# Second layer's attention: one matmul of 96 rows in place of three of 16 rows for the meta keys

## The chip, the cores and the metric

The kernel runs on one core of one Trainium2 chip. The metric is the device time of one execution in microseconds. A core has several engines that run side by side, each with its own queue of instructions in order: PE (TensorE, the matmuls; its weight loads are listed as PEld), DVE (VectorE), ACT (ScalarE), POOL (GpSimd) and SP (SyncE, which issues most of the DMAs). Matmul results land in PSUM, everything else on the chip lies in SBUF; both have 128 partitions, called rows here. A matmul sums over the rows of its two operands: the one that is loaded first as weights (`lhsT`) and the one that is streamed (`rhs`), one column after the other.

## The reference

The input is 512 tokens of width 1024, in front of which 16 learned meta tokens are put. Three layers follow: a gated delta rule, a latent attention with 16 heads, and a block with pooling, dilated attention and a feed-forward part. The change lies in the second, whose attention is:

```python
def causal_block_attention(q_nope, q_rope, k_nope, k_rope, v):
    ...
        s = (jnp.einsum('bqhd,bkhd->bhqk', qn_b, k_nope, preferred_element_type=jnp.float32)
             + jnp.einsum('bqhr,bkr->bhqk', qr_b, k_rope, preferred_element_type=jnp.float32))
        q_pos = blk * Q_BLOCK + jnp.arange(Q_BLOCK)
        s = jnp.where(q_pos[:, None] >= k_pos[None, :], s * scale, -jnp.inf)
        p = jax.nn.softmax(s, axis=-1)
        return jnp.einsum('bhqk,bkhd->bqhd', p.astype(v.dtype), v)
```

The keys are the 16 meta tokens and the 512 real ones. Keys and values of all heads come from one latent of width 128 (`c_kv`), so that the kernel can weigh the latent itself with the softmax weights and bring in each head's value matrix afterwards.

## The kernel before, in words

Everything is computed in full float32 precision by split products. A float32 tensor is cut in two by `cut` (line 75): ScalarE copies it into the matmuls' rounded float32 format (the high part), then VectorE subtracts that from the original (the low part). A product of two cut tensors is three matmuls into the same PSUM tile, `split_mm` (line 67): high by high (line 68), high by low (line 71), low by high (line 72). The fourth, low by low, is left out.

`Second.run` is the second layer. `latents` prepares the shared latent: beside the projections it is normalised, transposed in five chunks (the 16 meta tokens, then four times 128 tokens) and cut into `cthi` and `ctlo`, in which chunk 0 uses only rows 0 to 15.

Then the attention loop runs over 64 steps, 16 heads by 4 blocks of 128 queries. Different parts of it work on different steps at a time: `scores` on step i, `softmax_scale` on i - 1, `flip` on i - 2, `weigh` on i - 4 and `values` on i - 5, the last two once for two blocks (a half, 256 queries); `prep_a` and `prep_b` prepare the next head's queries.

- `scores`: matmuls into the PSUM tile `sc`; VectorE scales, masks and finds the extremum (line 1390), ScalarE takes the exponential (line 1395) into `p`; `softmax_scale` divides by the sum, on VectorE (line 1403) and GpSimd (line 1404).
- `flip`: PE transposes `p`, the 16 meta columns into `trm` (line 1726; a tile of which there is one, shared by the two blocks of a half) and the others into `ptr` (line 1729). These are cut into the pair `pt`, and `trm`, once both blocks are in it, into the pair `pm`, 16 rows by 256 queries.
- `weigh`: the latent weighed by the softmax weights. First the split product with the meta keys, three matmuls with 16 rows and 256 columns (`pm` by chunk 0 of `cthi`, `ctlo`), then the split products with the 2 or 4 blocks of real keys, 128 rows each, all into one PSUM tile. The result is cut into `oc`.
- `values`: `oc` by the head's value matrix, times the gate `sz`, cut into `ghi`/`glo`, the input of the layer's output projection.

Where the working tiles lie: `keep` is a pool that lives through the layer; `wk` is opened for the attention loop, after the pool with the layer's input (`h1hi`, `h1lo`) has been closed, on the same memory. `ones` is a constant tile of ones, 128x128.

The order of each engine's instructions is not that of the program text: when the kernel is built, a list scheduler orders them by the program's order as priority and by a simulated timeline (`schedule_with_timeline_sim=True`), except where the text keeps an order. So matmuls of `weigh`, `values`, `scores` and `flip` of neighbouring steps stand between one another in PE's queue.

Of the kernel before, what the change touches and what calls it, by code (L numbers as in the profile page):

```python
# [13 lines left out]
F32R = mybir.dt.float32r  # L14
AF = mybir.ActivationFunctionType
# [5 lines left out]
P = 128  # L21
D = 1024
KT = 8
META = 16
# [42 lines left out]
def split_mm(nc, ps, whi, wlo, xhi, xlo, start, stop, side=None):  # L67
    first = nc.tensor.matmul(ps, lhsT=whi, rhs=xhi, start=start, stop=False)  # L68
    if side is not None:
        side.hold(first)  # L70
    nc.tensor.matmul(ps, lhsT=whi, rhs=xlo, start=False, stop=False)  # L71
    nc.tensor.matmul(ps, lhsT=wlo, rhs=xhi, start=False, stop=stop)  # L72


def cut(nc, hi, lo, src, gain=None, engine=None):

    if gain is None:
        nc.scalar.activation(hi, src, AF.Copy)  # L78
        (engine or nc.vector).tensor_tensor(out=lo, in0=src, in1=hi.bitcast(F32), op=ALU.subtract)  # L79
    else:  # L80
        nc.scalar.activation(hi, src, AF.Copy, scale=gain)
        nc.vector.scalar_tensor_tensor(
            out=lo, in0=src, scalar=gain, in1=hi.bitcast(F32), op0=ALU.mult, op1=ALU.subtract
        )
# [1382 lines left out]
class Second:  # L1467
# [59 lines left out]
    def run(self, mixed):  # L1527
        e = self.e
        tc, nc, a, dram, pj, wts, ident, ones, vcol = (
            e.tc, e.nc, e.a, e.dram, e.pj, e.wts, e.ident, e.ones, e.vcol  # L1530
        )
# [10 lines left out]
        keep = ks_.enter_context(tc.tile_pool(reuse_waits="tile", name="l2", bufs=1, side="right"))  # L1542
# [3 lines left out]
        nc.scalar.dma_start(causal, a["causal"])  # L1546
        chi = keep.tile([P, T1], F32R, name="chi")
        clo = keep.tile([P, T1], F32R, name="clo")
        cthi = keep.tile([P, 5, P], F32R, name="cthi")
        ctlo = keep.tile([P, 5, P], F32R, name="ctlo")  # L1550
        khi = keep.tile([P, T1], F32R, name="krhi")
        klo = keep.tile([P, T1], F32R, name="krlo")
        nsc_q = keep.tile([P, 4], F32, name="nsc_q")
# [7 lines left out]
        def latents():  # L1561
            c = tp_.tile([P, T1], F32, tag="c1", name="c")
            sq = tp_.tile([P, T1], F32, tag="c2", name="csq")
            rc = tp_.tile([P, T1], F32, tag="c3", name="rc")
            nc.vector.tensor_tensor(out=c, in0=ckr[:, 0], in1=rs1, op=ALU.mult)
            nc.scalar.activation(sq, c, AF.Square)
            yield

            ps = tr_tile([P, 2, 4], "qms")
            for b in range(4):  # L1570
                bs = slice(P * b, P * b + P)
                nc.tensor.matmul(
                    ps[:, 0, b:b + 1], lhsT=acc[:, META + P * b:META + P * b + P], rhs=ones[:, 0:1], start=True, stop=True
                )
                for m in range(2):
                    nc.tensor.matmul(
                        ps[:, 1, b:b + 1], lhsT=lsq[:, m, bs], rhs=ones[:, 0:1], start=(m == 0), stop=(m == 1)
                    )
            t = tp_.tile([P, 2, 4], F32, name="qt")
            nc.vector.tensor_scalar(  # L1580
                out=t[:, 0], in0=ps[:, 0], scalar1=EPS / D, scalar2=EPS * EPS, op0=ALU.mult, op1=ALU.add
            )
            nc.vector.tensor_scalar(out=t[:, 1], in0=ps[:, 1], scalar1=1.0 / 256, scalar2=None, op0=ALU.mult)
            nc.vector.tensor_add(t[:, 1], t[:, 1], t[:, 0])
            nc.gpsimd.tensor_tensor(out=nsc_q, in0=t[:, 1], in1=e.half_pow, op=ALU.pow)
            nc.vector.tensor_scalar(out=nsc_q, in0=nsc_q, scalar1=-(192 ** -0.5), scalar2=None, op0=ALU.mult)
            yield
            for s in HALVES:
                token_rs(e, rc[:, s], sq, s, P, 1.0, gap=4.5)
            yield  # L1590
            yield
            nc.vector.scalar_tensor_tensor(
                out=rc, in0=c, scalar=vcol("kv_lat"), in1=rc, op0=ALU.mult, op1=ALU.mult
            )
            cut(nc, chi, clo, rc)
            yield
            for c in range(5):
                t0, n = CHUNKS[c]
                ws = slice(0, P) if c == 0 else slice(t0, t0 + P)
                ps = tr_tile([P, P], "ctp")  # L1600
                nc.tensor.transpose(ps, rc[:, ws], ident)
                cut(nc, cthi[0:n, c], ctlo[0:n, c], ps[0:n])
            yield

            kr = tp_.tile([P, T1], F32, tag="c1", name="kr")
            kx = tp_.tile([P, T1], F32, tag="c2", name="kx")
            nc.vector.tensor_tensor(out=kr, in0=ckr[:, 1], in1=rs1, op=ALU.mult)
            for b in range(4):
                o = b ^ 1
                nc.sync.dma_start(kx[32 * b:32 * b + 32], kr[32 * o:32 * o + 32])  # L1610
            sgn = tp_.tile([P, T1], F32, name="sgn")
            nc.scalar.dma_start(sgn, a["sin_signed"])
            yield
            nc.vector.tensor_mul(kr, kr, cos)
            nc.gpsimd.tensor_mul(kx, kx, sgn)
            yield
            nc.vector.tensor_add(kr, kr, kx)
            cut(nc, khi, klo, kr)
            yield
# [34 lines left out]
        def prep_b(h):  # L1654
# [6 lines left out]
            q_abs[h] = qa  # L1661

        side = latents()
        for h in range(16):
            if h in (2, 5, 8, 11):
# [32 lines left out]

        ws_ = ExitStack()
        wk = ws_.enter_context(tc.tile_pool(reuse_waits="tile", name="l2_work", bufs=2))  # L1700

        def scores(h, b):
            n = META + P * (b + 1)
            qs = slice(P * b, P * b + P)
            qa, qr = q_abs[h], qr_t[h // 4]
            sc = []
            for s in ([slice(0, n)] if n <= 512 else [slice(0, n // 2), slice(n // 2, n)]):
                ps = psm.tile([P, 512], F32, tag="sc", name="sc", bufs=2)[:, :s.stop - s.start]
                split_mm(nc, ps, qa[0][:, qs], qa[1][:, qs], chi[:, s], clo[:, s], True, False)
                nc.tensor.matmul(ps, lhsT=qr[:, h % 4, qs], rhs=khi[:, s], start=False, stop=False)  # L1710
                nc.tensor.matmul(ps, lhsT=qr[:, h % 4, qs], rhs=klo[:, s], start=False, stop=True)
                sc.append(ps)
            live[h, b] = softmax_exp(e, wk, sc, causal[:, T1 - n:], None, nsc_q[:, b:b + 1])

        def flip(h, b):

            p, _, _ = live.pop((h, b))
            half, j = divmod(b, 2)
            if j == 0:
                o = pts[h, half] = Env()  # L1720
                o.pt = [wk.tile([P, 4, 256], F32R, tag=f"pt{i}", name=f"pt{i}") for i in range(2)]
                o.pm = [wk.tile([META, 256], F32R, tag=f"pm{i}", name=f"pm{i}") for i in range(2)]
                o.tm = psm.tile([META, 256], F32, tag="trm", name="trm")
            o = pts[h, half]
            js = slice(P * j, P * j + P)
            nc.tensor.transpose(o.tm[:, js], p[:, 0:META], ident)
            tr = tr_tile([P, 4, P], "ptr")
            for k in range(b + 1):
                nc.tensor.transpose(tr[:, k], p[:, META + P * k:META + P * k + P], ident)  # L1729
            cut(nc, o.pt[0][:, 0:b + 1, js], o.pt[1][:, 0:b + 1, js], tr[:, 0:b + 1])  # L1730
            if j == 1:
                cut(nc, o.pm[0], o.pm[1], o.tm)

        def weigh(h, half):

            o = pts[h, half]
            ps = pj.tile([P, 512], F32, tag="pj", name="pj_t")[:, :256]
            split_mm(nc, ps, cthi[0:META, 0], ctlo[0:META, 0], o.pm[0], o.pm[1], True, False)
            nk = 2 * half + 2
            for k in range(nk):  # L1740
                s = slice(P if k == nk - 1 else 0, 256)
                split_mm(
                    nc, ps[:, s], cthi[:, k + 1], ctlo[:, k + 1], o.pt[0][:, k, s], o.pt[1][:, k, s], False, k == nk - 1
                )
            o.oc = [wk.tile([P, 256], F32R, tag=f"oc{i}", name=f"oc{i}") for i in range(2)]
            cut(nc, o.oc[0], o.oc[1], ps)
            o.sz = wk.tile([P, 256], F32, tag="sz", name="sz", bufs=3)
            nc.sync.dma_start(o.sz, sz_dram[h][:, SEQ_HALVES[half]])
# [9 lines left out]
        for i in range(len(steps) + 6):  # L1758
            if i < len(steps):
                scores(*steps[i])  # L1760
            if 0 <= i - 1 < len(steps):
                p, st, n = live[steps[i - 1]]
# [451 lines left out]
```

## Time and profile before

| | us |
|---|---|
| median of 3 runs | 1664.18 |
| lowest and highest of them | 1661.94, 1669.47 |
| the profiled execution | 1664.66 |
| its span, first to last instruction | 1662.8 |
| PE busy in the span | 1585.1 (95%) |
| VectorE busy | 985.6 (59%) |
| ScalarE busy | 834.5 (50%) |
| GpSimd busy | 434.2 (26%) |

The profile is one execution. Its views give, for each instruction, the start and the duration on its engine. For PE the durations overlap, since matmuls are pipelined: a matmul of 256 columns is listed with 0.28 us while the next one starts 0.12 us after it. Where the pace of PE is meant, the difference between two starts is read. The line numbers (L68) are those of the kernel; the tile names are written "out<-in", and "16*128 16x256" is a matmul with weights of 16 rows and 128 columns and a streamed operand of 16 rows and 256 columns.

### The profile page before, as it was taken

What the parts mean: (1) busy time and instruction counts of PE and PEld (TensorE: products, weight loads), DVE (VectorE), ACT (ScalarE), POOL (GpSimd) and SP (SyncE); (2) the same over time, 40 slices, a digit from 0 to 9 for tenths busy, and PEclk for the clock granted to TensorE, in tenths of its full rate; (3) what the DMA queues carried; (4) which work ended last, traced back from release to release, by engine and by line L of the source; (5) the groups of instructions that cost most, each with busy time, mean ns of one, the idle gap of its engine ahead of it and who ended that gap; (6) DMA issues with size and microseconds to landing.
All of it is one profiled execution on the core that took longest, in us unless ns stands there. A gap on an engine that the chain in (4) does not pass through costs nothing.

```text
span 1662.8 us, 32878 instructions
## 1 busy us (share of the span) xinstructions
PE 1585.1 (95%) x12564; PEld 1452.0 (87%) x12564; DVE 985.6 (59%) x1988; ACT 834.5 (50%) x1998; POOL 434.2 (26%) x640
## 2 busy tenths in 40 slices
PE   6999879999999999999999999999999999999997
PEld 6999768888889999878999899988889888888997
DVE  6847758655376477785676623767855645544133
ACT  4886645554487564434666533435864432332230
POOL 1112110111186631222444312324544111111110
PEclk9999979999999999999999999999999999999998
DMA  3247874424465563455221223485624223223332
GB/s 131 101 163 211 210 139 135 112 95 156 129 184 186 170 242 125 146 199 162 74 61 52 71 100 129 134 253 179 154 65 139 90 101 101 89 101 107 97 115 76
DMA packets 133361, 219.72 MB, mean 132 GB/s; under 512 B 35988, under 2 KB 81364, under 8 KB 133076
## 3 DMA queue, kind: packets, MB, share of 16 engines
q1 hardware_dynamic: 126436, 204.83, 39.7%
q10 hardware_dynamic: 6768, 12.79, 2.2%
q8 instruction: 99, 1.62, 0.4%
q14 instruction: 58, 0.48, 0.1%
HBM read 173.81 MB, written 42.45 MB: 130 GB/s over the span
## 4 chain that ended last, share of the span: by engine, by line
PE 74%; DMA 10%; DVE 6%; ACT 4%; issue 4%; POOL 1%; SPq 0%; POOLq 0%; ACTq 0%; DVEq 0%
PE pj_t L68 20%; PE pj_t L71 19%; PE pj_t L72 19%; DMA bca<-row_a 2%; DMA item_dram<-bca 1%; DVE wlo L79 1%; DMA bc<-row_b 1%; DMA raw<-w_z 1%; PE ptr L1729 1%; ACT whi L78 1%; PE first L68 1%; PE first L71 1%; PE sc L68 1%; PE first L72 1%; PE vtp L1143 1%
## 5 line engine op out<-in xcount | busy, mean ns | idle before, releaser
L79 DVE TENSOR_TENSOR wlo<-raw,whi 128x1024 fp32r<-128x1024 f32 (+2 forms) x218 | 291.2, 1336 | 226.6 <-ACT whi L78 222.8
L78 ACT ACTIVATE whi<-raw 128x1024 fp32r<-128x1024 f32 (+3 forms) x225 | 232.3, 1033 | 337.7 <-PE pj_t L71 190.0
L68 PE MATMUL pj_t<-hhi,whi 128*128 128x272 f32 (+2 forms) x760 | 224.9, 297 | 6.4 <-ACT y L726 2.3
L71 PE MATMUL pj_t<-hlo,whi 128*128 128x272 f32 (+2 forms) x760 | 224.8, 296 | 0.0
L72 PE MATMUL pj_t<-hhi,wlo 128*128 128x272 f32 (+2 forms) x760 | 224.0, 295 | 0.0
L68 PEld LDWEIGHTS pj_t<-hhi,whi 128*128 128x128 f32 (+1 forms) x760 | 145.8, 192 | 10.0 <-issue 2.6
L72 PEld LDWEIGHTS pj_t<-hhi,wlo 128*128 128x128 f32 (+1 forms) x760 | 145.8, 192 | 4.9 <-issue 4.3
L71 PEld LDWEIGHTS pj_t<-hlo,whi 128*128 128x128 f32 (+1 forms) x760 | 146.1, 192 | 2.5 <-issue 1.7
L72 PE MATMUL pj_t<-x3hi,wlo 128*128 128x512 f32 x320 | 125.4, 392 | 0.0
L71 PE MATMUL pj_t<-x3lo,whi 128*128 128x512 f32 x320 | 125.2, 391 | 0.0
L68 PE MATMUL pj_t<-x3hi,whi 128*128 128x512 f32 x320 | 125.2, 391 | 0.0
L361 POOL TENSOR_TENSOR acc<-acc,ysq 128x256 f32<-128x256 f32 (+1 forms) x48 | 59.1, 1231 | 195.5 <-ACT ysq L359 195.4
L68 PE MATMUL pj_t<-ahi,whi 128*128 128x256 f32 x352 | 99.3, 282 | 0.0
L72 PE MATMUL pj_t<-ahi,wlo 128*128 128x256 f32 x352 | 99.1, 282 | 0.0
L71 PE MATMUL pj_t<-alo,whi 128*128 128x256 f32 x352 | 99.1, 282 | 0.0
L1404 POOL TENSOR_SCALAR p<-p,st 128x144 f32<-128x144 f32 (+3 forms) x112 | 61.7, 553 | 133.4 <-DVE st L1403 98.3
L2104 POOL TENSOR_TENSOR gt<-gt,x3rs 128x512 f32<-128x512 f32 x22 | 30.9, 1405 | 192.9 <-DVE gt L2103 192.9
L68 PE MATMUL pj_t<-ghi,whi 128*128 128x272 f32 (+1 forms) x256 | 75.3, 294 | 0.0
L1395 ACT ACTIVATE p<-p,st 128x144 f32<-128x144 f32 (+3 forms) x112 | 63.1, 564 | 23.1 <-DVE st L1390 21.1
L730 DVE SCALAR_TENSOR_TENSOR y<-xpad,fixed,y 128x528 f32<-128x528 f32 x96 | 74.1, 774 | 0.6
L71 PE MATMUL pj_t<-glo,whi 128*128 128x272 f32 (+1 forms) x256 | 72.8, 284 | 0.0
L72 PE MATMUL pj_t<-ghi,wlo 128*128 128x272 f32 (+1 forms) x256 | 72.8, 285 | 0.0
(549 smaller groups left out, 4729.7 us busy)
## 6 DMA issues: line engine op xcount, KB each, us to landing
raw<-w_out SPq DMA_DIRECT2D x54, 512.0 KB, 3.7
raw<-w_z SPq DMA_DIRECT2D x32, 512.0 KB, 3.4
item<-item_dram SPq DMA_DIRECT2D x32, 384.0 KB, 3.1
raw<-w_v SPq DMA_DIRECT2D x22, 512.0 KB, 4.1
raw<-w_gate SPq DMA_DIRECT2D x22, 512.0 KB, 3.3
raw<-w_up SPq DMA_DIRECT2D x22, 512.0 KB, 3.2
sz<-sz_dram SPq DMA_DIRECT2D x64, 128.0 KB, 2.7
raw<-w_down SPq DMA_DIRECT2D x16, 512.0 KB, 3.6
```

Of the source, the lines that this page charges most:

```text
L68: first = nc.tensor.matmul(ps, lhsT=whi, rhs=xhi, start=start, stop=False)
L71: nc.tensor.matmul(ps, lhsT=whi, rhs=xlo, start=False, stop=False)
L72: nc.tensor.matmul(ps, lhsT=wlo, rhs=xhi, start=False, stop=stop)
L78: nc.scalar.activation(hi, src, AF.Copy)
L79: (engine or nc.vector).tensor_tensor(out=lo, in0=src, in1=hi.bitcast(F32), op=ALU.subtract)
L361: eng.tensor_tensor(out=acc[:, s], in0=acc[:, s], in1=sq[:, :n], op=ALU.add)
L730: nc.vector.scalar_tensor_tensor(out=y, in0=xpad[:, j:j + T1], scalar=cw[:, tap0, j:j + 1], in1=y, op0=ALU.mult, op1=ALU.add)
L1143: nc.tensor.transpose(tp[:, r], vT[r][:, win(c)], ident)
L1395: nc.scalar.activation(p[:, :at], p[:, :at], AF.Exp, bias=st[:, len(sc) - 1:len(sc)], scale=-1.0, accum_out=st[:, 3:4])
L1404: nc.gpsimd.tensor_scalar(out=p[:, :n], in0=p[:, :n], scalar1=st[:, 2:3], scalar2=factor, op0=ALU.mult, op1=ALU.mult)
L1729: nc.tensor.transpose(tr[:, k], p[:, META + P * k:META + P * k + P], ident)
L2104: nc.gpsimd.tensor_tensor(out=gt, in0=gt, in1=rs, op=ALU.mult)
```

## The change

The three matmuls with the meta keys become one with 96 rows. Its streamed operand holds three copies of the softmax weights: the high part on rows 0 to 15, the low part on rows 32 to 47, the high part again on rows 64 to 79. Its weights hold, on the same rows, the high part of the latent, the high part again, and its low part. The sum over the rows is then the sum of the three products. The rows between are zero in both.

To that end: the weights `cm` are a tile of their own, zeroed once by ScalarE and filled from chunk 0 by a cut and one more ScalarE copy, while `cthi` and `ctlo` shrink to the four chunks of real keys. The streamed operands are two fixed tiles `pms`, one for each half of the queries, in place of pairs from a rotating pool; each is zeroed once by two ScalarE instructions ahead of the attention loop. In `flip` the cut writes rows 0 to 15 and 32 to 47, and one more ScalarE copy writes rows 64 to 79, 32 times in all.

```diff
-        cthi = keep.tile([P, 5, P], F32R, name="cthi")
-        ctlo = keep.tile([P, 5, P], F32R, name="ctlo")
+        cthi = keep.tile([P, 4, P], F32R, name="cthi")
+        ctlo = keep.tile([P, 4, P], F32R, name="ctlo")
+
+        cm = keep.tile([3 * 32, P], F32R, name="cm")
+        nc.scalar.activation(cm, ones[0:3 * 32], AF.Copy, scale=0.0)
...
-                cut(nc, cthi[0:n, c], ctlo[0:n, c], ps[0:n])
+                if c == 0:
+                    cut(nc, cm[0:n], cm[64:64 + n], ps[0:n])
+                    nc.scalar.activation(cm[32:32 + n], ps[0:n], AF.Copy)
+                else:
+                    cut(nc, cthi[:, c - 1], ctlo[:, c - 1], ps)
...
+        pms = [wk.tile([3 * 32, 256], F32R, name=f"pm{i}", bufs=1) for i in range(2)]
+        for pm in pms:
+            for i in range(2):
+                nc.scalar.activation(pm[:, P * i:P * i + P], ones[0:3 * 32], AF.Copy, scale=0.0)
...
-                o.pm = [wk.tile([META, 256], F32R, tag=f"pm{i}", name=f"pm{i}") for i in range(2)]
+                o.pm = pms[half]
...
-                cut(nc, o.pm[0], o.pm[1], o.tm)
+                cut(nc, o.pm[0:META], o.pm[32:32 + META], o.tm)
+                nc.scalar.activation(o.pm[64:64 + META], o.tm, AF.Copy)
...
-            split_mm(nc, ps, cthi[0:META, 0], ctlo[0:META, 0], o.pm[0], o.pm[1], True, False)
+            nc.tensor.matmul(ps, lhsT=cm, rhs=o.pm, start=True, stop=False)
...
-                    nc, ps[:, s], cthi[:, k + 1], ctlo[:, k + 1], o.pt[0][:, k, s], o.pt[1][:, k, s], False, k == nk - 1
+                    nc, ps[:, s], cthi[:, k], ctlo[:, k], o.pt[0][:, k, s], o.pt[1][:, k, s], False, k == nk - 1
```

## Rows read from the trace of the kernel before

**Rows 1.** The page: PE's busy us, share, instructions; PE's granted clock in 40 slices.

```profile
PE 1585.1 (95%) x12564; PEld 1452.0 (87%) x12564; DVE 985.6 (59%) x1988; ACT 834.5 (50%) x1998; POOL 434.2 (26%) x640
...
PEclk9999979999999999999999999999999999999998
```

**Rows 2.** Table by stretch: length, busy us per engine (PE first), clock, DMA.

```profile
774.80:948.80 174.00, 173.02 (x1236) 155.51 (x1235) 122.27 (x405) 113.06 (x316) 67.71 (x98) 1.00 0.21 62
```

**Rows 3.** Waits of PE in that stretch: who for whom, us, times, longest.

```profile
PE trm L1726 <- DVE pm L79: 0.8, 1, 0.8
```

**Rows 4.** Instructions that touch pm: count, shortest/median/longest ns, first and last start.

```profile
L68 PE MATMUL pj_t<-pm,cthi x32: 378/381/386, 775.9 to 947.1; 16*128 16x256 f32 x32
```

**Rows 5.** Timeline of PE, one set: start us, duration us, what.

```profile
800.53 0.28 PE L71 MATMUL pj_t<-oc,whi 128*128 128x256 f32 x1
800.65 0.28 PE L72 MATMUL pj_t<-oc,wlo 128*128 128x256 f32 x1
800.86 0.38 PE L68 MATMUL pj_t<-pm,cthi 16*128 16x256 f32 x1
801.08 0.27 PE L71 MATMUL pj_t<-pm,cthi 16*128 16x256 f32 x1
801.20 0.28 PE L72 MATMUL pj_t<-pm,ctlo 16*128 16x256 f32 x1
801.40 0.39 PE L68 MATMUL pj_t<-pt,cthi 128*128 128x256 f32 x1
801.63 0.28 PE L71 MATMUL pj_t<-pt,cthi 128*128 128x256 f32 x1
```

**Rows 6.** Timeline of the weight loads, the same set.

```profile
800.42 0.19 PEld L71 LDWEIGHTS pj_t<-oc,whi 128*128 128x128 f32 x1
800.53 0.19 PEld L72 LDWEIGHTS pj_t<-oc,wlo 128*128 128x128 f32 x1
800.85 0.18 PEld L68 LDWEIGHTS pj_t<-pm,cthi 16*128 16x128 f32 x1
```

**Rows 7.** Timeline of PE, a set whose first product stands apart.

```profile
794.57 0.28 PE L72 MATMUL pj_t<-oc,wlo 128*128 128x256 f32 x1
794.78 0.38 PE L68 MATMUL pj_t<-pm,cthi 16*128 16x256 f32 x1
...
795.41 0.38 PE L71 MATMUL pj_t<-pm,cthi 16*128 16x256 f32 x1
...
796.06 0.38 PE L1729 MATMUL ptr<-fixed,p 128*128 128x128 f32 x2
```

**Rows 8.** Timeline of PE in the first layer: products of 16 and of 32 rows.

```profile
342.64 0.28 PE L1186 MATMUL vn<-vb,nu 16*16 16x128 f32 x1
342.66 0.26 PE L1032 MATMUL y_ps<-td,nu 32*32 32x32 f32 x6
```

**Rows 9.** Timeline of ScalarE: the copy of trm and the next instruction.

```profile
804.12 0.37 ACT L78 ACTIVATE pm<-trm 16x256 fp32r<-16x256 f32 x1 [1.08 <-PE trm L1726]
804.40 0.61 ACT L1395 ACTIVATE p<-p,st 128x400 f32<-128x400 f32 x1
```

**Rows 10.** Timelines of ScalarE and VectorE: both write parts of vv, third layer.

```profile
1079.08 0.47 ACT L81 ACTIVATE vv<-pj_t,rq 128x256 fp32r<-128x256 f32 x1 [2.21 <-PE pj_t L72]
...
1079.27 0.87 DVE L82 SCALAR_TENSOR_TENSOR vv<-pj_t,rq,vv 128x256 fp32r<-128x256 f32 x2
```

**Rows 11.** Timelines of VectorE and PE: the subtraction, then trm's next transposes.

```profile
804.53 0.41 DVE L79 TENSOR_TENSOR pm<-trm,pm 16x256 fp32r<-16x256 f32 x1 [0.47 <-ACT pm L78]
...
807.14 0.28 PE L1726 MATMUL trm<-fixed,p 128*16 128x128 f32 x1
807.35 0.39 PE L71 MATMUL pj_t<-pm,cthi 16*128 16x256 f32 x1
```

**Rows 12.** Timelines of ScalarE and PE at the head of the stage.

```profile
767.97 0.60 ACT L78 ACTIVATE qa<-pj_t 128x512 fp32r<-128x512 f32 x1 [2.40 <-PE pj_t L72]
...
768.01 0.39 PE L72 MATMUL pj_t<-h1hi,wlo 128*128 128x512 f32 x1
```

## What is predicted for the change, and why

> **What bounds the kernel now.** I read the page first: PE's line of the busy table and the slices of its clock [rows 1]. PE is busy for 95% of the span, and the clock stands at full speed in nearly every slice. The change touches the second layer's attention, so the next view is the table by stretch for that stage alone, from the first cut of transposed weights at 774.8 us to the last matmuls of the last head at 948.8 us [rows 2]. It is 174.0 us long; PE is busy for 173.0 of them at a granted clock of 1.00 (the level of 2.4 GHz), while VectorE has 122.3 us of work and ScalarE 113.1. The waits of PE in the same stretch come to one wait of 0.8 us [rows 3]. So here PE does not wait for others: what is taken from PE's stream ends the stage earlier, until another engine is the slower one.
>
> A busy PE need not be streaming columns, so the last view is the timeline of PE in order of time, where I read starts, not durations. Two matmuls of 256 columns on all 128 rows stand 0.12 us apart: 800.53 to 800.65 [rows 5]. The three products with the meta keys (16 rows) do not keep that pace.
>
> **The matmuls removed.** There are 32 of the first of the three meta products, one for each head and half of the queries [rows 4], and as many of the second and of the third. Two of the three go: 64 matmuls.
>
> **The breaks around them.** In the common form the three stand together behind 128-row matmuls and ahead of 128-row matmuls [rows 5]. From the start of the last 128-row matmul before (800.65) to the start of the second one behind (801.63) is 0.98 us for five intervals; at the pace of 0.12 it would be 0.60. The 0.38 over lies where the row count changes: 0.21 and 0.22 on going in, 0.20 and 0.23 on coming out, and 0.12 between the second and the third meta product, which have the same rows. The weight loads show the same [rows 6]: the first load with 16 rows begins 0.32 us behind the load before it, against 0.11 to 0.12 between loads of 128 rows. With one product of 96 rows and no break there would be three intervals, 0.36 us. That saves 0.98 - 0.36 = 0.62 us. I count 24 sets of this form in the timeline of the stage: 24 x 0.62 = 14.9 us.
>
> In the other 8 sets the first meta product stands alone, other work follows, and the other two come later [rows 7]. There PE changes over four times: from 794.57 to 796.06 it took 1.49 us for seven intervals. Without breaks and with two matmuls fewer these are three intervals of 0.12 and two of 0.11 (the transposes), 0.58 us. That saves 0.91, eight times 7.3 us. Together 22.2 us, of which 64 x 0.12 = 7.7 us are matmuls and 14.5 us are breaks.
>
> **Does a product of 96 rows still break the stream?** No row of before shows one, so this is bounded from both sides: the break stays (0.38 us for each set) or it is gone. Two rows speak for gone. In the first layer a product of 16 rows and one of 32 rows stand 0.02 us apart, 342.64 and 342.66 [rows 8]: unequal row counts alone don't break the stream, so what changes must be a coarser setting that 16 and 32 rows share and 16 and 128 don't. 96 rows need three quarters of the array, as near to 128 as any here. I take gone.
>
> The Trainium skill agrees with the row: TensorEngine Tiling, Tiling Modes, has modes of 128, 64 and 32 rows and says that changing the mode drains the engine; 96 rows fit only the whole array. Another page speaks against this change: TensorE: Matmul & The Clock Gate, Packing small matmuls, has weight loads overlap matmuls in flight only where the row groups differ. By that rule the 16-row loads would be the cheap ones, and only the 7.7 us of matmuls would be saved. The loads of this trace don't agree: 128-row loads overlap each other's matmuls, the 16-row load waits [rows 6].
>
> **What ScalarE gets.** Each set adds one ScalarE copy of 16x256 out of PSUM. The like copy takes 0.37 us, but the next instruction starts 0.28 us after it [rows 9]; 32 of them are 9.0 to 11.8 us. ScalarE's work becomes 113.1 + 11.8 = 124.9 us in a stage of about 152: 82%. It stays below PE. Queued behind the copy on ScalarE are an exponential, a cut of the transposed weights or of the head's output; PE comes to these later by at most the 0.28 us, and most of their waits have more room. Were the copy made to wait for VectorE's subtraction into the same tile, ScalarE would stand still for as long as that takes. Two parts of one tile are written by both engines in the third layer, and there ScalarE wrote its part at 1079.08 while VectorE only began on its own at 1079.27 [rows 10], so I put that wait at nothing.
>
> The one product also waits for all three parts, where before the first matmul needed only ScalarE's high part. Nothing is lost by that: between the end of VectorE's subtraction and the second meta matmul, which needs it already, there are 0.4 to 6.2 us, half of them over 4 us; 804.94 to 807.35 is one [rows 11]. What PE waits for more than now I bound by nothing below and by half of the gain, 11 us, above; PE waits for 0.8 us today at 70% and 65% on the two other engines [rows 2, 3], so I take 1.5 us.
>
> **What is put in at the head of the stage.** Four ScalarE writes of zeros (96x128) stand ahead of the first scores. Their space is that of the layer's input, which PE reads until 768.01 + 0.39 = 768.40 us; ScalarE idles for 2.40 us before 767.97 and is then busy nearly without a break until the first exponential [rows 12]. At 0.25 us each, the step between two short copies [rows 9], they push that chain by 1.0 us if nothing covers it, by nothing if they fall into a gap. I take 1.0. The zeros and the extra copy for the key side come once, in the stage before, beside the projections; two copies are 0.6 us there, off the path. Memory only gets smaller. No DMA is added or moved, on no queue.
>
> **The sum.** The profiled execution took 1664.7 us, its span 1662.8, 0.5 us over the median of the three times. 1664.7 - 22.2 + 1.0 + 1.5 = 1645.0, against the median 1644.5 us. The stages behind start earlier by as much; the next one begins with PE busy for all of its time, so nothing there gives it back. The order of every engine is chosen anew when the kernel is built, so small things move elsewhere too; I allow 3 us either way.
>
> **Rivals.**
> (1) 96 rows break the stream as 16 do. Saved are the 7.7 us of matmuls, and the second pair of breaks in the 8 split sets, half of 1.49 - 0.82 (seven intervals without breaks) each: 8 x 0.34 = 2.7. 10.4 - 2.5 = 7.9 us: 1656.3. For it: 96 isn't 128, and no row shows one. Against: rows 8.
> (2) The gain is there, but PE now waits for ScalarE and VectorE, at about 82% each, through the softmax chain or through the outputs' cuts: half of it is lost, 1655.5. For it: many short steps from engine to engine. Against: PE's waits today [rows 3].
> (3) Slower: the one PSUM buffer of the transposed meta weights (trm). It was free when VectorE had subtracted; now it is free when ScalarE's second copy has run as well, and PE, which works in order, stands at the next transposes into it. Today 0.2 to 4.2 us lie between, the median 2.7; one is 804.94 to 807.14 [rows 11]. If the copy lands in ScalarE's queue behind two or three long ones, PE stands. The gain is used up when the wait is 22.2 / 32 = 0.7 us in the mean, so when the copy ends 3.4 us behind the subtraction; at 1.0 us in the mean it is 32 - 22.2 = 10 us slower: 1674. For it: PE's one wait today is this very one. Against: the copy needs nothing but the transposes, and stands next to the high part's copy in the program.
> (4) The weight loads of 16 rows cost nothing extra, and the breaks are something else that stays around the set in all its forms: 7.7 - 2.5 = 5.2 saved, 1659.0. For it no row; against it rows 6. It is what the second of the two rules above would give.
>
> **How the numbers follow.** Chances: the forecast 0.73, rival 1 0.12, rival 2 0.08, rival 3 0.05, rival 4 0.02. The predicted time is 1644.5. The range goes down to 1638 (neither of the two costs of 2.5, 0.8 us of wait gone, the 3 us of other stages) and up to 1657, which takes in rivals 1 and 2. A measurement of this kernel tells a change from none at about 0.5%, 8.3 us, so faster is below 1655.9: the forecast and somewhat under half of rivals 1 and 2 are faster (0.82), the rest of these and rival 4 the same (0.13), rival 3 slower (0.05).
>
> **What would show it.** In PE's timeline after: one meta matmul of 96 rows in each set, 0.12 us from either neighbour; if it stands 0.2 us from both, rival 1. The stage's stretch: about 152 us with PE still busy throughout; 163 us would be rival 1, and idle time of PE with waits for ScalarE or VectorE rival 2. Waits of PE at trm for a ScalarE copy would be rival 3. The forecast is wrong above all if the break goes with any row count other than 128.

## The result, and the profile after

The changed kernel takes 1647.5 us (median of four runs) against 1663.1 us beside it: a ratio of 0.989, with a 95% interval of 0.987 to 0.991. A second comparison (below, with other runs of both) gave 0.986, 0.984 to 0.988. The prediction was 1644.5 us, 1638 to 1657, which is 19.7 us less than the kernel before; the two comparisons measured 15.6 and 21.3 us less. They differ in the kernel before, whose median was 1663.1 us in the first and 1669.9 us in the second, while the changed kernel took 1647.5 and 1648.6 us; why the kernel before took longer there no profile shows.

The page of the changed kernel, PE's busy time and its clock, which answer to [rows 1]:

```profile
PE 1565.5 (95%) x12500; PEld 1441.5 (88%) x12500; DVE 985.0 (60%) x1988; ACT 845.5 (51%) x2036; POOL 437.6 (27%) x640
...
PEclk9999988999999999999999999999999999999999
```

PE has 64 matmuls fewer and 19.6 us less of busy time, ScalarE 38 instructions more: 32 copies, the 4 zero writes of the stage and two for the key side.

To compare whole stages I take the attention from its first scores matmul to the last matmul with `oc` as its input. The table by stretch gives, for the kernel before (columns as in [rows 2]):

```profile
768.85:952.75 183.90, 182.15 (x1300) 163.89 (x1300) 126.63 (x417) 118.10 (x327) 71.58 (x101) 1.00 0.23 68
```

and for the changed one:

```profile
774.66:939.66 165.00, 161.26 (x1237) 153.23 (x1236) 127.81 (x417) 128.72 (x363) 71.51 (x101) 1.00 0.26 76
```

The stage went from 183.9 to 165.0 us, 18.9 us less; the prediction had 22.2 - 2.5 = 19.7. PE's busy time in it fell by 20.9 us (182.15 to 161.26), and its idle time rose from 1.75 to 3.74 us. ScalarE's work grew by 10.6 us, VectorE's by 1.2. The stage begins 5.8 us later than before, because the first layer took longer in that execution. The same stretch of the first layer, before, after, and in a repeat of the changed kernel:

```profile
17.60:449.40 431.80, 405.51 (x4736) 376.20 (x4737) 272.35 (x505) 250.55 (x622) 60.68 (x150) 0.97 0.49 140
```

```profile
17.90:455.10 437.20, 411.49 (x4736) 380.76 (x4737) 273.19 (x504) 250.69 (x622) 60.59 (x150) 0.96 0.49 138
```

```profile
17.90:448.00 430.10, 407.06 (x4736) 377.42 (x4737) 272.22 (x504) 250.71 (x622) 60.31 (x150) 0.98 0.49 140
```

It has the same 4736 matmuls each time and takes 431.8, 437.2 and 430.1 us: this part differs from one execution to the next by some 7 us, whatever the kernel. The granted clock goes with it: 0.97, 0.96 and 0.98 in the three rows, the longest stretch at the lowest clock. In the stage of the attention the clock was 1.00 in both kernels, and its length was 165.00 and 165.02 us in two executions of the changed kernel. So in what follows the stage's length is what tells variants apart where its clock is 1.00, and the total time only where they differ by more than this spread. Each other variant was profiled once, and the scheduler chose its order anew, so that differences of a few tenths of a us between variants are less sure than the repeat of one kernel suggests.

PE's timeline in a set, which answers to [rows 5]:

```profile
849.08 0.28 PE L72 MATMUL pj_t<-oc,wlo 128*128 128x256 f32 x1
849.20 0.28 PE L1750 MATMUL pj_t<-pm,cm 96*128 96x256 f32 x1
849.32 0.28 PE L68 MATMUL pj_t<-pt,cthi 128*128 128x256 f32 x1
849.43 0.28 PE L71 MATMUL pj_t<-pt,cthi 128*128 128x256 f32 x1
```

The one meta matmul stands 0.12 us from either neighbour; from the matmul before to the second one behind it is 0.35 us, where it was 0.98. What PE waits for in the stage now, the longest of eight lines, 3.4 us in all; over the whole stage the kernel before has the wait of [rows 3] and two more, 1.5 us in all:

```profile
PE ptr L1740 <- POOL p L1404: 1.0, 1, 1.0
PE sc L68 <- DVE st L1390: 0.5, 1, 0.5
PE pj_t L68 <- ACT oc L78: 0.5, 1, 0.5
PE pj_t L1750 <- ACT pm L1744: 0.5, 1, 0.5
PE trm L1737 <- ACT pm L1744: 0.3, 1, 0.3
```

### The profile page after: what moved, and what is told of

Its sections match the earlier page's. It is cut to its first block, busy times and chain, and to the rows that moved or that the text cites. A ratio compares the mean times of both kernels' runs of the same rounds, so it can differ in the third digit from the quotient of the medians.

```text
span 1646.4 us, 32795 instructions
## 1 busy us (share of the span) xinstructions
PE 1565.5 (95%) x12500; PEld 1441.5 (88%) x12500; DVE 985.0 (60%) x1988; ACT 845.5 (51%) x2036; POOL 437.6 (27%) x640
## 4 chain that ended last, share of the span: by engine, by line
PE 72%; DMA 8%; DVE 7%; issue 5%; ACT 5%; POOL 2%; SPq 0%; POOLq 0%; ACTq 0%; DVEq 0%
PE pj_t L68 19%; PE pj_t L71 19%; PE pj_t L72 19%; DVE wlo L79 1%; DMA raw<-w_z 1%; PE ptr L1740 1%; DMA item_dram<-bca 1%; DMA resid<-h_w_out 1%; DMA item<-item_dram 1%; DVE y L403 1%; DMA sp_q<-rot_c 1%; DVE y L730 1%; PE sc L68 1%; PE vtp L1143 1%; ACT whi L78 1%
## 5 line engine op out<-in xcount | busy, mean ns | idle before, releaser
L79 DVE TENSOR_TENSOR wlo<-raw,whi 128x1024 fp32r<-128x1024 f32 (+2 forms) x218 | 287.9, 1321 | 228.7 <-ACT whi L78 224.8
L1395 ACT ACTIVATE p<-p,st 128x144 f32<-128x144 f32 (+3 forms) x112 | 63.2, 565 | 22.2 <-DVE st L1390 17.5
```

Of the source, the lines that this page charges most:

```text
L1395: nc.scalar.activation(p[:, :at], p[:, :at], AF.Exp, bias=st[:, len(sc) - 1:len(sc)], scale=-1.0, accum_out=st[:, 3:4])
```

## The experiments

### The changed kernel again, and its two parts taken apart

First the changed kernel once more, unaltered.

> The changed kernel once more, beside the three that follow. In the first profile the attention stage (first scores matmul to last value matmul) went from 183.9 to 165.0 us, 18.9 less, while the first layer, which has the same instructions in both, took 5.7 us longer in that one execution. If the first layer's difference is only one execution against another, the stage is again about 165 us, the first layer comes out anywhere within some 6 us, and the time is 1646 to 1650 us. If the change itself had lengthened the first layer, it is again 5 to 6 us longer there.

Measured: 1648.6 us, the first layer 430.1 us (its row stands above), and the stage:

```profile
770.58:935.60 165.02, 161.27 (x1236) 153.22 (x1236) 127.78 (x417) 128.75 (x363) 71.51 (x101) 1.00 0.27 76
```

The longer first layer of the first profile was one execution's.

Then three matmuls as before, but each with operands that zeros fill up to 96 rows. The row count is what changes for PE; beside it the operands are fixed tiles, as in the changed kernel, with eight writes of zeros at the head of the stage, and there is no third copy:

```diff
+        cms = [keep.tile([3 * 32, P], F32R, name=f"cm{i}") for i in range(2)]
+        for cm in cms:
+            nc.scalar.activation(cm, ones[0:3 * 32], AF.Copy, scale=0.0)
...
-            split_mm(nc, ps, cthi[0:META, 0], ctlo[0:META, 0], o.pm[0], o.pm[1], True, False)
+            split_mm(nc, ps, cms[0], cms[1], o.pm[0], o.pm[1], True, False)
```

> The three meta products stay three matmuls, with the operands of each padded by zeros to 96 rows; no third copy. My theory: 14.5 us of the 22.2 lay in the breaks between 16-row and 128-row matmuls, 7.7 in the two matmuls, so this one gains 14.5 less 1 to 2 us for eight zero writes at the head: 1650 to 1651 us, the stage about 171 us, each meta matmul 0.12 us from its neighbours. Rival: the breaks belong to having three small products there and not to their row count, or 96 rows break the stream too: no gain, 1663 us, with starts 0.2 us apart at both ends of the set.

Measured: 1656.4 us against 1669.9 us, a ratio of 0.991 (0.988 to 0.993). The 13.5 us less are what was expected; the 1650 to 1651 us were not met, since they started from the first comparison's time of the kernel before. The timeline of PE in a set, and below it the stage in the table by stretch:

```profile
841.31 0.28 PE L72 MATMUL pj_t<-oc,wlo 128*128 128x256 f32 x1
841.43 0.29 PE L68 MATMUL pj_t<-pm,cm 96*128 96x256 f32 x1
841.55 0.28 PE L71 MATMUL pj_t<-pm,cm 96*128 96x256 f32 x1
841.68 0.28 PE L72 MATMUL pj_t<-pm,cm 96*128 96x256 f32 x1
841.80 0.28 PE L68 MATMUL pj_t<-pt,cthi 128*128 128x256 f32 x1
841.92 0.29 PE L71 MATMUL pj_t<-pt,cthi 128*128 128x256 f32 x1
```

```profile
779.47:950.67 171.20, 168.42 (x1300) 159.93 (x1300) 124.69 (x417) 118.00 (x335) 71.28 (x101) 1.00 0.26 74
```

The five intervals take 0.61 us here (the median of the 24 such sets is 0.60), where the 16-row products took 0.98 [rows 5]. Nothing else differs within such a set, so the 0.38 us is the price of the row count. The stage is 171.2 us: 12.7 us less with the same 1300 matmuls. PE's busy time fell by 13.7 us, against 14.5 that the prediction had for the breaks, and its idle time rose by 1.0. The other 6.2 us come from the two matmuls that go, less what the third copy costs.

### Which row counts break the stream

One matmul as in the changed kernel, which reads only the first 16, 64 or 80 of its rows. With 16 only high by high is computed, with 64 two of the three terms; with 80 nothing is left out, since rows 80 to 95 are zero.

```diff
-            nc.tensor.matmul(ps, lhsT=cm, rhs=o.pm, start=True, stop=False)
+            nc.tensor.matmul(ps, lhsT=cm[0:64], rhs=o.pm[0:64], start=True, stop=False)
```

> The changed kernel, but its one matmul reads only rows 0 to 15 (high by high); the two smaller terms of the meta product are left out, everything else is done, the copies too. It isolates the break at one matmul for each set. If 16 rows among 128 break the stream at every set, as the three 16-row products did (0.98 us where 96 rows gave 0.60), a set takes 0.36 + 0.38 = 0.74 us from the matmul before to the second one behind, and the stage 165.0 + 32 x 0.38 = about 177 us. If a break needs several small products in a row, it is 0.36 us and 165 us.

> The same with rows 0 to 63 (two terms, the third is left out). If what matters is a setting that 16, 32 and 64 rows each differ in from 128, as the first layer's intervals on going from 64 to 128 rows suggest (0.15 us and then 0.22), a set takes about 0.74 us and the stage about 177 us, as with 16 rows. If only 32 rows and fewer are a class apart, 0.36 us and 165 us.

> The changed kernel with the matmul cut to rows 0 to 79, all that is not zero: nothing is left out. If every count from 65 on runs in the setting of 128 rows, a set takes 0.36 us and the stage 165.0 us, to 0.2 us the changed kernel. If 96 is free of breaks only because it is whole groups of 32 rows, 0.74 us and about 177 us.

PE's timeline in a set with 16, with 64 and with 80 rows:

```profile
821.95 0.28 PE L68 MATMUL pj_t<-oc,whi 128*128 128x256 f32 x1
822.16 0.38 PE L1750 MATMUL pj_t<-pm,cm 16*128 16x256 f32 x1
822.47 0.39 PE L68 MATMUL pj_t<-pt,cthi 128*128 128x256 f32 x1
822.69 0.28 PE L71 MATMUL pj_t<-pt,cthi 128*128 128x256 f32 x1
```

```profile
842.13 0.28 PE L72 MATMUL pj_t<-oc,wlo 128*128 128x256 f32 x1
842.34 0.38 PE L1750 MATMUL pj_t<-pm,cm 64*128 64x256 f32 x1
842.65 0.39 PE L68 MATMUL pj_t<-pt,cthi 128*128 128x256 f32 x1
842.88 0.28 PE L71 MATMUL pj_t<-pt,cthi 128*128 128x256 f32 x1
```

```profile
841.35 0.28 PE L72 MATMUL pj_t<-oc,wlo 128*128 128x256 f32 x1
841.47 0.29 PE L1750 MATMUL pj_t<-pm,cm 80*128 80x256 f32 x1
841.59 0.28 PE L68 MATMUL pj_t<-pt,cthi 128*128 128x256 f32 x1
841.71 0.28 PE L71 MATMUL pj_t<-pt,cthi 128*128 128x256 f32 x1
```

The stages in the table by stretch, in the same order (with 16 rows its last 30 us ahead of the whole):

```profile
920.00:949.75 29.75, 27.48 (x172) 24.07 (x172) 17.04 (x51) 16.91 (x47) 9.39 (x14) 0.89 0.23 71
...
770.80:949.75 178.95, 175.82 (x1236) 158.35 (x1236) 127.87 (x417) 130.83 (x363) 72.61 (x101) 0.98 0.24 70
```

```profile
774.14:948.77 174.63, 172.72 (x1237) 156.36 (x1236) 127.67 (x417) 130.26 (x363) 71.42 (x101) 1.00 0.25 72
```

```profile
771.84:936.86 165.02, 161.26 (x1236) 153.24 (x1236) 127.75 (x417) 128.86 (x363) 71.51 (x101) 1.00 0.26 76
```

From the matmul before to the second one behind: 0.74 us with 16 rows, 0.75 with 64, 0.36 with 80. A break of 0.38 us is paid once for each visit, whether one product or three are made on it, and 16 and 64 rows pay the same. 80 rows pay none, so it isn't the whole groups of 32 either. The stages follow, 174.6 with 64 rows and 165.0 with 80 (these three kernels were timed in one execution each, 1661.7, 1661.5 and 1648.8 us). With 64 rows the stage is 9.6 us longer than in the changed kernel and not the expected 32 x 0.38 = 12.2: PE is busy for 11.5 us more and idle for 1.8 us less (1.91 us in place of 3.74), so a part of the breaks takes the place of waits. With 16 rows the stage is 179.0 us, but there the granted clock fell to 0.89 in its last 30 us, so its length can't be set beside the others; the set shown lies ahead of that. This settles rival 1 (96 rows break the stream too: no) and rival 4 (the breaks stay around the set in all its forms: with 80 and 96 rows they are gone, and with 16 and 64 they are there).

### What the third copy costs

In the changed kernel the third copy waits for VectorE. Its timeline on ScalarE, and VectorE's subtraction ahead of it:

```profile
800.45 0.41 DVE L79 TENSOR_TENSOR pm<-trm,pm 16x256 fp32r<-16x256 f32 x1
...
800.90 0.37 ACT L1744 ACTIVATE pm<-trm 16x256 fp32r<-16x256 f32 x1 [0.71 <-DVE pm L79]
```

In all 32 sets it starts 0.03 to 1.52 us after the subtraction has ended. So in the next kernel the copy was put ahead of the subtraction:

```diff
-                cut(nc, o.pm[0:META], o.pm[32:32 + META], o.tm)
+                nc.scalar.activation(o.pm[0:META], o.tm, AF.Copy)
                 nc.scalar.activation(o.pm[64:64 + META], o.tm, AF.Copy)
+                nc.vector.tensor_tensor(
+                    out=o.pm[32:32 + META], in0=o.tm, in1=o.pm[0:META].bitcast(F32), op=ALU.subtract
+                )
```

> The changed kernel with the third copy written ahead of VectorE's subtraction in the program. In the trace of the changed kernel that copy started 0.03 to 1.52 us after the subtraction had ended in all 32 sets, so ScalarE does wait for it. If that wait costs little, because PE waits for the copy for only 1.1 us in the stage, this one is 0.5 to 1.5 us faster than the changed kernel (stage 163.5 to 164.5 us). If the 3.3 us that the stage fell short of the gross 22.2 are this wait and what queues behind it, it is 3 us faster (stage 162 us).

In another, the zeros were written early, in the pool `keep`, and the copy left where it was:

> The changed kernel with the two streamed tiles taken from the pool that lives through the layer and zeroed some 110 us earlier, beside the projections. If the four zero writes at the head of the stage push the chain of the first exponentials, as I put at 1.0 us, the stage is 0.5 to 1.0 us shorter (164.0 to 164.5 us). If ScalarE's gap before the table load hides them, it is 165.0 us as before. Total time within 0.1% of the changed kernel in both cases.

Then both together, and at last, starting from the kernel with both, the copy on GpSimd, which reads the high part in SBUF:

```diff
-                nc.scalar.activation(o.pm[64:64 + META], o.tm, AF.Copy)
+                nc.gpsimd.tensor_copy(o.pm[64:64 + META], o.pm[0:META])
```

> The changed kernel with the third copy ahead of the subtraction and the zeros early. Alone they shortened the stage by 0.7 and 0.4 us. If the two act in different places they add up: 163.9 us, the time 1 us under the changed kernel's. If the scheduler's new order gives one of them back, 164.3 to 165 us.

> Zeros early, and the third copy made by GpSimd out of SBUF (from the high part, rows 0 to 15, to rows 64 to 79), so that ScalarE has no more work in the stage than before the change and the PSUM buffer is free when the subtraction has run. If ScalarE's copy is what the stage lost against the gross 22.2 us, the stage is 162 to 163 us; if the loss is in the shorter distance between all steps, whoever copies, or if GpSimd's copy comes late and PE waits for it, 164 to 166 us.

The stage of each, in this order:

```profile
771.08:935.37 164.29, 161.16 (x1236) 153.23 (x1236) 127.34 (x417) 127.64 (x363) 71.99 (x101) 1.00 0.27 77
```

```profile
778.74:943.35 164.61, 161.28 (x1236) 153.24 (x1236) 127.79 (x417) 127.84 (x359) 71.55 (x101) 1.00 0.27 76
```

```profile
776.20:940.10 163.90, 161.19 (x1237) 153.24 (x1237) 127.36 (x417) 126.96 (x359) 72.27 (x101) 1.00 0.27 77
```

```profile
774.51:937.66 163.15, 160.75 (x1236) 152.91 (x1236) 129.11 (x417) 116.82 (x327) 85.16 (x133) 1.00 0.27 77
```

By these rows the wait for VectorE costs 0.7 us, the zeros at the head 0.4, both add up to 1.1, and taking the copy off ScalarE altogether gives 0.75 more: 163.15 us (the second and the fourth are 0.1 to 0.2 us above the ranges expected). In total time none of the four can be told from the changed kernel: their ratios are 0.985, 0.988, 0.989 and 0.988, with intervals of about 0.002 either way that meet those of the changed kernel, 0.989 and 0.986. The first has a median of 1646.9 us. The three with early zeros have 1652.5, 1652.4 and 1650.7 us, above the changed kernel's 1647.5 and 1648.6 and above the 0.1% that had been expected of early zeros alone; whether that is the spread of the rest of the kernel or a cost of the early zeros stays open. No faster kernel has been shown.

With GpSimd the copy and the subtraction write different rows of `pm` and ran at the same time in 17 of 32 sets; the first is one:

```profile
781.27 0.39 POOL L1744 CAST pm<-pm 16x256 fp32r<-16x256 f32 x1 [1.81 <-ACT pt L78]
...
781.34 0.41 DVE L1745 TENSOR_TENSOR pm<-trm,pm 16x256 fp32r<-16x256 f32 x1
```

With the copy on ScalarE and first, VectorE's subtraction never began before the copy's end (0.03 us after it at the least). So the tile that both write isn't what holds the second of the two there. What is left is the PSUM buffer that ScalarE's copy and the subtraction both read, and GpSimd's copy doesn't. That agrees with [rows 10], where the same two engines write parts of one tile out of different PSUM tiles and don't wait; the GpSimd kernel changes the engine as well, so by itself it doesn't show it.

### How much ScalarE has left

Two more ScalarE copies were put into the text of each set, into scratch, first from the PSUM buffer of the transposes, then from an SBUF tile:

```diff
+                for i in range(2):
+                    extra = wk.tile([META, 256], F32, tag="extra", name="extra")
+                    nc.scalar.activation(extra, o.tm, AF.Copy)
```

> The changed kernel with two more ScalarE copies of the same transposes into scratch in every set, 64 in all, some 18 us of work for ScalarE. ScalarE has 128.7 us of work in the stage of 165.0 now. If the copies are covered and PE stays the bound, the stage grows by 0.5 to 3 us, as the first copy did (the stage fell 3.3 us short of the gross gain). If ScalarE is already about to be the bound, through its in-order queue, the stage grows by 10 us or more.

> The changed kernel with two more ScalarE copies of 16x256 in every set, as in the run before, but from a tile in SBUF and not from the one PSUM buffer of the transposes. The two extra copies from the buffer made the stage 23.8 us longer (188.8 against 165.0). If that was ScalarE's load and its queue, the stage is again 180 to 190 us. If it was the buffer, held until the last copy, it is 165 to 170 us.

The stage in the table by stretch and PE's longest waits in it, first for the copies from the buffer:

```profile
773.54:962.34 188.80, 173.31 (x1237) 155.94 (x1237) 128.14 (x417) 147.96 (x427) 71.39 (x101) 1.00 0.24 67
```

```profile
PE pj_t L1753 <- ACT pm L1744: 8.4, 14, 0.9
PE sc L68 <- DVE st L1390: 2.7, 8, 0.5
```

and for those from SBUF, the whole stage and its first 60 us, and below it the 64 copies with their first and last start:

```profile
771.86:943.13 171.27, 164.40 (x1237) 153.62 (x1237) 128.30 (x417) 144.88 (x427) 71.23 (x101) 1.00 0.26 73
771.86:831.86 60.00, 56.13 (x400) 50.72 (x399) 41.59 (x140) 59.54 (x186) 22.75 (x31) 1.00 0.26 71
```

```profile
L1747 ACT ACTIVATE extra<-chi x64: 396/400/418, 774.0 to 830.2; 16x256 f32<-16x256 f32 x64
```

The copies from the buffer make the stage 23.8 us longer, more than the whole gain (one execution: 1673.7 us); those from SBUF make it 6.3 us longer (1654.9 us), which lies in neither of the two ranges expected. The two don't set the same load beside each other, though. The copies from SBUF need nothing, and the scheduler put all 64 into the first 58 us of the stage, where ScalarE was busy for 59.5 of 60 us; those from the buffer lie two by two in all 32 sets. So 6.3 us is the price of a ScalarE with hardly a gap for a third of the stage, and how much of the 23.8 us is load and how much comes with the buffer isn't shown. That load alone makes up the 23.8 us is unlikely: in that kernel ScalarE was busy for 51.1 of the first 60 us and for 96.8 of the 128.8 behind them, a smaller share than 59.5 of 60.

With the copies from the buffer, PE's main wait is the meta matmul for the third copy, which stands ahead of the two extra ones. It starts 0.05 us behind that copy in 22 of 32 sets, in the changed kernel in 2, and the 32 visits, from the matmul before to the second one behind, take 26.2 us in place of 13.0. PE's wait for the buffer itself, which is where I had put rival 3, isn't in the list. The scheduler gave PE another order in this kernel; that a buffer planned as busy for longer moves the transposes nearer to the matmul that needs them is my reading of it and wasn't tried.

## Why the prediction was right, step by step

**What bounds the stage.** Right: with 64 matmuls and all breaks gone PE is busy for 161.3 of 165.0 us, and the gain in the stage is 85% of the gross sum (18.9 of 22.2). It isn't busy throughout, as the prediction had it: it is idle for 2.0 us more than before, and the stretch of [rows 2], for which it had about 152 us, took 155 (780.65 to 935.80).

**The matmuls and the breaks.** Right, set by set. A set in the common form went from 0.98 to 0.36 us (predicted 0.36), and the two parts were seen apart: 0.38 for the breaks, 0.24 for two matmuls. In sum PE's busy time fell by 20.9 us of the 22.2. The bound that no row of before could close, whether 96 rows break the stream, fell on the side that the 16- and 32-row products of the first layer had pointed to [rows 8].

**The two rules on rows.** The Trainium skill, TensorEngine Tiling, Tiling Modes, says that a change of the mode drains the engine and knows 128, 64 and 32 rows: these runs agree, with 0.38 us for going in and out of a product of 16 or of 64 rows, and none for 80 and 96. The overlap of weight loads only for different row groups (the Trainium skill, TensorE: Matmul & The Clock Gate, Packing small matmuls), read as the prediction read it, would have made the padding to 96 rows useless; the padded kernel gained 12.7 us in the stage.

**The head of the stage.** Put at 1.0 us, the upper of its bounds; 0.4 measured. The zeros push the chain ahead of the first exponential, as I had it, but they stand 0.2 us apart and not 0.25 (rows 9, named for it, show 0.28), and part of them falls into the 0.39 us for which ScalarE stood idle there before.

**The third copy.** Here a step failed, though the total came out right. I put the wait of the copy for VectorE at nothing, since in the third layer ScalarE and VectorE write parts of one tile without waiting [rows 10]. Those two read different PSUM tiles at that time; the copy and the subtraction read the same one, and the second does wait. It cost only 0.7 us: in 29 of the 32 sets ScalarE had other work until within 0.03 us of the copy's start, and in the other three it stood idle for 1.2 us in all. The copy's place on ScalarE costs 0.75 us more.

**What the sum missed.** 22.2 - 18.9 = 3.3 us were lost in the stage: 0.4 for the zeros, 0.7 for the wait, 0.75 for the copy's place on ScalarE, and 1.45 that remain in the version with GpSimd. There PE has six waits of 0.2 to 0.5 us, for three different engines; whether that rest has one cause stays open. So the costs behind the head came to 2.9 us where 1.5 were allowed, and the head to 0.4 where 1.0 was: the two errors partly cancel, which is luck.

**Rival 3** didn't come. The slack between the buffer's last reader and its next transposes, 2.7 us in the median before, is 1.4 in the changed kernel, and PE waited there once, for 0.3 us. Two more copies of 0.37 us from the buffer turn the gain into a loss, but not by this mechanism: the slack is then 2.1 us, and PE's waits are at the meta matmul.

**The total.** The prediction was 3 us low: 0.8 of it is the stage (18.9 against 19.7), the rest is no more than what other stages vary by between executions. What the runs confirm is the forecast of the stage. That the total came within 3 us is in part luck, since the gain over the kernel before was 15.6 us in one comparison and 21.3 in the other.

## What to carry to other kernels

Before costing matmuls by their columns, read PE's starts where the row count changes: a visit to a product of 16 or of 64 rows among 128-row ones cost 0.38 us here, more than three matmuls of 256 columns, and a product of 80 or 96 rows, partly zeros, cost none of it. Where the terms of a split product leave rows free, stacking them on one operand saves the matmuls as well, but look at who must write the second copy and what it reads: two more reads of the PSUM buffer a set cost 23.8 us here, more than the matmuls gave, even if the cause of that is open. When parts of a kernel vary between executions by more than the change is worth, compare the length of the stage that was changed.

## What was not expected of the hardware

That 16 and 64 rows pay the same 0.38 us at 2.4 GHz, and 80 the same nothing as 96. And how little the load of ScalarE says by itself: with 59.5 of 60 us busy it cost 6.3 us, while two reads more of one PSUM buffer a set cost 23.8 us, though ScalarE was then idle for a fifth of the stage (148.0 of 188.8 us busy).
